# A backward list schedule that ranks every instruction by its latest start, in a planner that orders a two-layer decoder step

## The chip, the cores and the metric

The kernel runs on one core of one Trainium2 chip. The metric is the device time of one execution in microseconds (us), the median of several runs. A core has five engines that each work through a queue of their own in order: TensorE (PE) for matmuls and transposes, with its weight load shown apart as PEld; VectorE (DVE); ScalarE (ACT); GpSimd (POOL); and SyncE (SP), which here issues nearly all DMA transfers. An instruction waits at the head of its queue until what it needs is there, and everything behind it on that engine waits too.

## The reference

One inference step of a decoder with two layers, for a prompt of 2048 tokens and 8 sample tokens that share the weights; the width is 1024, all in float32:

```python
def even_mixer(x, past_kv, w_in, w_sp, b_sp):            # layer 0: branches A and B
    h = jnp.einsum('btd,de->bte', x, w_in)
    u, v, gate_a, q, k, vb, gate_b = _split(h, EVEN_SPLITS)
    u = jax.nn.gelu(u)
    v = _standardize(jax.nn.gelu(v)).astype(x.dtype)
    out_a = chunk_spatial_gate(u, v, w_sp, b_sp) * jax.nn.silu(gate_a)
    ...
    o = sweep_query_blocks(lambda qs, pos: stick_breaking(qs[0], keys, vals, pos, k_pos), (q,), q_pos)
    out_b = o.reshape(b, t, BRANCH_WIDTH) * jax.nn.silu(gate_b)
    return jnp.concatenate([out_a, out_b], axis=-1), new_kv, v

def odd_mixer(...):                                       # layer 1: branches C and D
    ...
    o = sweep_query_blocks(lambda qs, pos: dsa_attend(...), (q, q_idx, w_idx), q_pos)
    out_c = o.reshape(b, t, BRANCH_WIDTH) * jax.nn.silu(gate_c)
    out_d = multiscale_pool(p_ext, n_pref, q_pos, w_grp, scale) * jax.nn.silu(gate_d)
    return jnp.concatenate([out_c, out_d], axis=-1), new_kv, k_idx, new_buf

def post_norm(x, h, w_o, g, b):
    return _layer_norm(DN_ALPHA * x + jnp.einsum('bte,ed->btd', h, w_o), g, b)
```

`stick_breaking` is attention with 8 heads of 64 whose weights are running products of 1 − sigmoid(z) over the keys. `dsa_attend` lets an indexer with 4 heads of 32 score all keys, keeps the 256 best of each query, and does softmax attention over those with 8 query heads on 2 key heads and a relative bias. Both are causal for the prompt and read a paged cache for the samples. Each layer has one input projection, one output projection and a LayerNorm behind the residual.

## The kernel before

The prompt is worked on in 4 blocks of 512 tokens (TB), each of four tiles (P = 128 tokens). `Body` writes the program as generators for the stages and runs them interleaved, so that the order in which the code is written already mixes the stages of several blocks. What it writes is not what runs: `Order` takes the finished list of instructions, gathers what each depends on (`gather`), lays them on the five engines by a list schedule with planned durations (`cost`, `plan`), and pins the order that comes out on each engine (`keep`). In `plan` an instruction is ready when what it reads is done and its tile has a buffer; of the ready ones an engine takes the one that comes first in the program. The buffers of a tag (a name of a tile) are given out in program order. Waits between engines are set by the data alone; the planned durations are used only to choose the order.

The names in the rows below:

- `xc` are activations on their way in (a DMA on SP, L436); PE transposes them (`ps_x`, L439), and ACT and DVE split the result into a high part `xh` (L376) and a low part `xl` (L382). Weights `wr` (L387) are split in the same way into `wh` (ACT, L389) and `wl` (POOL and DVE, L392). A projection `pp` is three matmuls, high × high, low × high and high × low (L463 to L465). `q_hl` and `k_hl` are queries and keys after the same split by L382.
- Branch A: `wsp` are its four spatial weights (L507 to L511). Branch B: scores `z` (L753), a scan on DVE over `P` (L767), transposes `ps_p` (L790) and the sums `av` (L799).
- Branch C: the indexer's scores `z_i` (L1185), the search for the 256th best score (`tk_` names, to L1291), a mask `mk`. Then, for each tile of queries and each head, scores `z_c` of 128 queries by up to 512 keys in PSUM (L1495, two matmuls each). One DVE instruction (L1497) adds the mask, takes the largest (`mx`) and writes the sum as `zt` in SBUF, which frees the PSUM bank. ACT takes the exponential of `zt` (L1513). PE transposes it (`ps_pc`, L1526), ACT copies it back (L1528), and PE multiplies by the values into `av_c` (L1540, output tiles of 64 rows, the "halves" of the code). At the end of a tile of queries `c_sum` is scaled, multiplied by `av_c` and by the gate `gc` on DVE (L1564, L1568), and stored to `otd` on SP (L1571). The last tile is split instead (`lh`, `ll`).
- The output projection `pp_o` is again three matmuls, of `oh` and `ol` by the weights (L858 to L860, for the last tile L893 to L895); DVE adds it to the residual `xres` (L863, L897).
- LayerNorm (`ln_late`, `ln`): statistics, then for each of two halves of 512 columns and each of four tiles a multiply-add on DVE (L940), a product with `lng` on POOL (L941), a sum with `lnb` on DVE (L942), and the store (L909).

The scores `z`, `z_c` and `z_i` share one pool of two PSUM banks; `pp`, `ps_x`, `pp_o` and others share another; transposes a third.

Of the kernel before, what the change touches and what calls it, by code (L numbers as in the profile page):

```python
# [20 lines left out]
P = 128  # L21
# [34 lines left out]
class Order:  # L56

    ENGINES = {"PE": "PE", "DVE": "DVE", "Activation": "ACT", "Pool": "POOL", "SP": "SP"}
    SEM, DMA_START, DMA_END, RATE = 150, 700, 1500, 280.0

    def __init__(self, tc, lags):
# [44 lines left out]
    def gather(self):  # L106
# [3 lines left out]
        for n, i in enumerate(self.ins):  # L110
# [7 lines left out]
            for w, x in list(self.operands(i)):  # L118
# [74 lines left out]
    def cost(self, n):  # L193
# [22 lines left out]
        if e == "PE":  # L216
            k = self.size(i.outs[0])
            if i.is_transpose:
                return 90, 250
            if i.ins[0].dtype == F32R:  # L220
                return max(58, 0.444 * k), 0.444 * k + 170
            w = tuple(i.tile_size)[1] / P if self.halves(n) else 1.0
            return max(132, 1.7 * k * w), max(222, 1.7 * k) + 170
# [21 lines left out]
    def halves(self, n):  # L245
# [3 lines left out]
                and tuple(i.tile_size)[1] < P)  # L249


    def plan(self):

        N, eng, push, pop = len(self.ins), self.eng, heapq.heappush, heapq.heappop
        cost, halves = [self.cost(n) for n in range(N)], [self.halves(n) for n in range(N)]
        for g, ms in self.group.items():
            busy = sum(cost[m][0] for m in ms)
            cost[g] = busy, busy + 170
        dma = [e is not None and "DMA" in i.opcode for e, i in zip(eng, self.ins)]
        left, succ, tiles, home = [len(d) for d in self.dep], [[] for _ in range(N)], [[] for _ in range(N)], {}  # L260
        for n, d in enumerate(self.dep):
            for m in d:
                succ[m].append(n)
        for g, ts in self.tags.items():
# [8 lines left out]
        users = {t: len(u) for t, u in self.uses.items()}  # L273
        since, done = [0.0] * N, [0.0] * N
        ready, idle = {e: [] for e in self.ENGINES.values()}, dict.fromkeys(self.ENGINES.values(), 0.0)
        self.order = {e: [] for e in ready}
        due, back, now, dma_end, half, count = [], [], 0.0, 0.0, False, 0

# [6 lines left out]
        def take(g, t):  # L285
            while queue[g] and free[g] and open_[g]:
                x = queue[g].pop()
                free[g] -= 1
                open_[g] = False
                for n in self.uses[x]:  # L290
                    release(n, t)
# [6 lines left out]
        while count < N:  # L298
            while back and back[0][0] <= now:
                g = pop(back)[1]  # L300
                free[g] += 1
                take(g, now)
            while due and due[0][0] <= now:
                n = pop(due)[1]
                if eng[n] is not None:
                    push(ready[eng[n]], n)
                    continue
                count += 1
                for m in succ[n]:
                    release(m, now)  # L310
            moved = False
            for e, q in ready.items():
                while q and idle[e] <= now:
                    n = pop(q)
# [4 lines left out]
                    if dma[n]:  # L319
# [10 lines left out]
                    for t in tiles[n]:  # L330
# [7 lines left out]
                        if not users[t]:  # L338
                            push(back, (max(done[m] for m in u) + self.SEM, g))
# [4 lines left out]
        return max(done)  # L344

    def keep(self):
# [1839 lines left out]
def build(nc, shapes):  # L2186
    I = {n: nc.dram_tensor(n, s, d, kind="ExternalInput").ap() for n, s, d in shapes}
    O = {n: nc.dram_tensor("out_" + n, s, F32, kind="ExternalOutput").ap() for n, s in _OUTS}
    with tile.TileContext(nc, schedule_with_timeline_sim=True) as tc:
# [4 lines left out]
        order.gather()  # L2194
        order.plan()
        order.keep()
# [13 lines left out]
```

## Time and profile before

| | |
|---|---|
| median of 3 runs | 3044.42 us (3036.56 to 3045.0) |
| profiled execution | 3043.16 us |
| its span | 3041.5 us |
| mean granted clock of TensorE | 0.953 |
| PE busy | 2764.8 us |
| DVE busy | 2194.6 us |
| ACT busy | 1565.6 us |
| POOL busy | 1093.9 us |
| DMA | 523.50 MB, mean 172 GB/s |

The span runs from the first to the last instruction. The granted clock is what the throttle left of TensorE's full speed, as a mean over the span. In the views of the profile each row of waits has the engine and line that waited, what released it, the total us, how often, and the longest. A row of the timeline has the start, the duration, the engine and line, the operation with output and inputs, the number of instructions that the row holds together and, in brackets, how long the engine sat idle before it and what ended that.

### The profile page before, as it was taken

How to read it: one execution, taken by the hardware profiler on the slowest of the kernel's cores; microseconds unless marked ns; L12 is line 12 of the kernel's file. 1: busy time of each engine (PE TensorE's matmuls, PEld its weight loads, DVE VectorE, ACT ScalarE, POOL GpSimd, SP SyncE). 2: the span in 40 equal slices, each digit the busy share in tenths (PEclk: the TensorE clock that was granted, in tenths of full speed). 3: DMA queues.
4: the chain of work that ended last, by engine and by line, in shares of the span. 5: the costliest groups of instructions: out<-in, count | busy, mean ns of one | idle time of the engine just before them, and what ended most of it. 6: DMA issues, size and time to landing. Idle time of an engine off the chain costs nothing. (4 is left out here: it accounts for less than half of the span.)

```text
span 3041.5 us, 52342 instructions
## 1 busy us (share of the span) xinstructions
PE 2764.8 (91%) x17490; PEld 2189.1 (72%) x17490; DVE 2194.6 (72%) x5493; ACT 1565.6 (51%) x3148; POOL 1093.9 (36%) x1172
## 2 busy tenths in 40 slices
PE   7998999889999889979699999998899998988986
PEld 6886678667777767767477677767777887876875
DVE  2466557757775786548888988896888778778765
ACT  2433333334444334435366676774576675666842
POOL 2323235432324532242323422234322655434342
PEclk9999999999999999989799999998989998998998
DMA  7556866777585667454665555425555655665452
GB/s 215 161 177 205 256 185 184 241 215 211 163 259 160 204 212 233 128 151 115 178 166 148 143 140 148 114 74 152 161 156 140 198 179 169 201 201 180 125 171 66
DMA packets 536591, 523.50 MB, mean 172 GB/s; under 512 B 43183, under 2 KB 408904, under 8 KB 536287
## 3 DMA queue, kind: packets, MB, share of 16 engines
q1 hardware_dynamic: 526439, 484.29, 53.7%
q0 software_dynamic: 9856, 35.66, 3.7%
q8 instruction: 138, 2.26, 0.3%
q14 instruction: 158, 1.29, 0.1%
HBM read 430.27 MB, written 89.73 MB: 171 GB/s over the span
## 5 line engine op out<-in xcount | busy, mean ns | idle before, releaser
L392 POOL TENSOR_TENSOR wl<-wr,wh 128x512 fp32r<-128x512 f32 x260 | 411.5, 1583 | 972.6 <-ACT wh L389 884.7
L463 PE MATMUL pp<-xh,wh 128*128 128x512 f32 (+1 forms) x1536 | 636.2, 417 | 22.6 <-DVE q_hl L382 15.0
L464 PE MATMUL pp<-xl,wh 128*128 128x512 f32 (+1 forms) x1536 | 616.8, 402 | 0.1
L465 PE MATMUL pp<-xh,wl 128*128 128x512 f32 (+1 forms) x1536 | 613.1, 399 | 0.8 <-DMA ksc<-kcs 0.6
L389 ACT CAST wh<-wr 128x1024 fp32r<-128x1024 f32 x260 | 269.9, 1038 | 367.1 <-PE pp L464 202.8
L392 DVE TENSOR_TENSOR wl<-wr,wh 128x512 fp32r<-128x512 f32 x260 | 231.6, 891 | 199.3 <-ACT wh L389 183.5
L463 PEld LDWEIGHTS pp<-xh,wh 128*128 128x128 f32 (+1 forms) x1536 | 288.4, 189 | 101.7 <-issue 20.0
L465 PEld LDWEIGHTS pp<-xh,wl 128*128 128x128 f32 (+1 forms) x1536 | 289.4, 188 | 66.9 <-issue 7.4
L464 PEld LDWEIGHTS pp<-xl,wh 128*128 128x128 f32 (+1 forms) x1536 | 290.3, 189 | 63.9 <-issue 13.0
L858 PE MATMUL pp_o<-wh,oh 128*128 128x256 f32 x1008 | 300.9, 300 | 22.9 <-ACT oh L376 16.1
L860 PE MATMUL pp_o<-wh,ol 128*128 128x256 f32 x1008 | 291.9, 293 | 7.7 <-POOL ol L382 7.5
L859 PE MATMUL pp_o<-wl,oh 128*128 128x256 f32 x1008 | 291.5, 290 | 1.5 <-POOL wl L392 1.4
L767 DVE TENSOR_TENSOR_SCAN P<-P,bfst 128x512 f32<-128x512 f32 x192 | 265.8, 1392 | 35.4 <-ACT P L760 35.1
L1495 PE MATMUL z_c<-ksc,qc 128*128 128x512 f32 (+3 forms) x816 | 231.5, 370 | 65.0 <-DVE mx L1497 53.4
L791 ACT COPY P<-ps_p 128x512 f32<-128x512 f32 (+1 forms) x320 | 166.9, 523 | 184.4 <-PE ps_p L790 176.6
L1528 ACT COPY zt<-ps_pc 128x512 f32<-128x512 f32 (+3 forms) x320 | 164.1, 520 | 159.9 <-PE ps_pc L1526 154.1
L1513 ACT ACTIVATE zt<-zt,nmax 128x512 f32<-128x512 f32 (+3 forms) x320 | 208.4, 653 | 71.3 <-DVE nmax L1501 70.8
L858 PEld LDWEIGHTS pp_o<-wh,oh 128*128 128x128 f32 x1008 | 196.7, 195 | 34.4 <-ACT oh L376 17.8
L1482 POOL TENSOR_TENSOR nm<-nm,mk 128x256 f32<-128x256 f32 (+1 forms) x128 | 97.1, 760 | 342.8 <-DMA nm<-bft 158.5
L1495 PEld LDWEIGHTS z_c<-ksc,qc 128*128 128x128 f32 x816 | 141.7, 203 | 105.7 <-DVE mx L1497 65.1
L1241 ACT ACTIVATE mk<-ix,tk_tn 128x384 int8<-128x384 f32 (+13 forms) x140 | 183.4, 1310 | 54.9 <-DVE tk_tn L1291 30.3
L753 PE MATMUL z<-ks,q 128*128 128x512 f32 (+3 forms) x640 | 193.5, 390 | 13.2 <-ACT P L760 4.6
(456 smaller groups left out, 5913.5 us busy)
## 6 DMA issues: line engine op xcount, KB each, us to landing
pg<-cache_b_kv SPq DMA_DIRECT2D x256, 256.0 KB
wr<-w_in_even SPq DMA_DIRECT2D x112, 512.0 KB
wr<-w_in_odd SPq DMA_DIRECT2D x76, 512.0 KB
wr<-w_out SPq DMA_DIRECT2D x68, 512.0 KB
ks<-ksc SPq DMA_DIRECT2D x80, 256.0 KB
ksc<-kcs SPq DMA_DIRECT2D x80, 256.0 KB
q<-qsc SPq DMA_DIRECT2D x64, 256.0 KB
qc<-qcs SPq DMA_DIRECT2D x128, 128.0 KB
```

Source lines behind the costliest of these rows:

```text
L389: nc.scalar.copy(hi, raw)
L392: e.tensor_tensor(lo[:, c], raw[:, c], hi[:, c].bitcast(F32), op=OP.subtract)
L463: nc.tensor.matmul(ps[:m], wh[:, kt, :m], xh[kt], start=a, stop=False)
L464: nc.tensor.matmul(ps[:m], wh[:, kt, :m], xl[kt], start=False, stop=False)
L465: nc.tensor.matmul(ps[:m], wl[:, kt, :m], xh[kt], start=False, stop=b)
L753: nc.tensor.matmul(z[:, :n], q2[:, c, t * P:(t + 1) * P].bitcast(F32R), ks[:, :n].bitcast(F32R), start=c == 0, stop=c == 1)
L767: nc.vector.tensor_tensor_scan(r, r, r, initial=ini, op0=OP.mult, op1=OP.bypass)
L858: nc.tensor.matmul(ps[:, :256], oh[:, tt], wh[:, k], start=a, stop=False)
L859: nc.tensor.matmul(ps[:, :256], oh[:, tt], wl[:, k], start=False, stop=False)
L860: nc.tensor.matmul(ps[:, :256], ol[:, tt], wh[:, k], start=False, stop=b)
L1495: nc.tensor.matmul(z[:, :n], q2[:, c, jj % 2, :].bitcast(F32R), kk, start=c == 0, stop=c == 1)
L1513: nc.scalar.activation(zt, zt, AF.Exp, bias=nmx, accum_out=st["rs"][:, h, c:c + 1])
```

## The change

Four things change in `Order`; `Body` is untouched, and so are the instructions.

1. The planned durations: transposes 107 instead of 90 ns, float32r matmuls, halves and other matmuls a little different, POOL's tensor-tensor a bit longer with float32r output, and a figure of its own for a DVE tensor-scalar with two outputs.
2. On PE a change of kind (transpose, float32r, halves, other) costs the planner 45 ns, or 100 where halves are on one side. Before, only a change to or from halves cost 100.
3. Reads of one PSUM tile by the same engine keep their program order.
4. The plan is made three times. The first goes by program order, as before. Then `latest` runs a list schedule backwards from the end: every instruction is placed as late as its users, its engine and the buffers of the last plan allow. The starts that come out are the ranks by which the next forward plan chooses among ready instructions. The plan that the planner itself finds shortest is kept; here it is the one after the second backward pass.

```diff
@@ class Order
+    KIND, TILED = 45, 100
@@ gather: PSUM reads by the same engine
                 if w:
                     dep[n].update(m for m, g in rs if hit(g))
+                elif own and self.space(x) == PSUM:
+                    dep[n].update(m for m, g in rs if self.eng[m] == self.eng[n])
                     if own and self.space(x) != DRAM:
@@ cost
             if i.is_transpose:
-                return 90, 250
+                return 107, 270
             if i.ins[0].dtype == F32R:
-                return max(58, 0.444 * k), 0.444 * k + 170
...
+                return max(60 if tuple(i.tile_size)[1] < P else 88, 15 + 0.422 * k), 0.444 * k + 170
...
-            c = {"TensorTensor": 150 + 2.45 * k, "Iota": 50 + 0.9 * k, "Memset": 40}.get(i.opcode, 330 + 0.9 * k)
+            c = {"TensorTensor": 150 + (2.85 if i.outs[0].dtype == F32R else 2.4) * k, "Iota": 50 + 0.9 * k, "Memset": 40}.get(i.opcode, 330 + 0.9 * k)
...
+        elif i.opcode == "TensorScalarPtr" and len(i.outs) > 1 and len(full) == 1:
+            c = 150 + 1.05 * k
...
+    def settle(self):
...
+        best = self.plan(list(range(N))), self.order
+        for _ in range(2):
+            best = min(best, (self.plan(self.latest()), self.order), key=lambda x: x[0])
+        self.order = best[1]
...
@@ plan(self, rank)
-                    push(ready[eng[n]], n)
+                    push(ready[eng[n]], (rank[n], n))
...
-                    if e == "PE" and halves[n] != half:
-                        half = not half
-                        s += 100
+                    if e == "PE" and kinds[n] != kind:
+                        s += self.TILED if "h" in (kinds[n], kind) else self.KIND
+                        kind = kinds[n]
...
+    def latest(self):
...
+        for a in range(N):
+            for b in self.succ[a]:
+                edge(a, b, 1.0 if eng[a] == eng[b] == "PE" else lat[a] if eng[a] is not None else 0.0)
+        for t, u in self.uses.items():
...
+            for m in self.uses[self.after[t]] if t in self.after else ():
+                edge(m, u[0], lat[m])
...
+        def release(b):
+            for a, lag in pred[b]:
+                since[a] = max(since[a], start[b] + cost[b][0] + lag - cost[a][0])
+                left[a] -= 1
+                if not left[a]:
+                    push(due, (since[a], -a))
...
+        return [-s - c[0] for s, c in zip(start, cost)]
...
@@ build
-        order.plan()
+        order.settle()
```

`after` holds, for each tile, the tile whose buffer it took over in the last plan, so that the backward pass knows that the old tile's users must be done before the new one's first. The lines of `Body` move down by 86 (L1497 is now L1583, L940 is L1026).

What it moves is shown at three places. At the start, on SP, the queue begins before with two weights and constants:

```order
L387 DMA wr_110<-w_in_even 128x8x128
L387 DMA wr_117<-w_in_even 128x8x128
L957 DMA dsc_147<-d_scale 128x4x1
L959 DMA dwg_149<-d_w_grp 128x4x128
L1149 DMA tkc_165<-tk_const 128x32
L500 DMA pg_191<-page_table 1x128
L504 DMA bb_197<-a_b_sp 128x512
L507 DMA wsp_199<-a_w_sp 128x128
...
L1582 DMA x_smp_329<-x_sample 8x1024
L436 DMA xc_344<-x_prompt 128x4x128
```

and now:

```order
L593 DMA wsp_199<-a_w_sp 128x128
L593 DMA wsp_205<-a_w_sp 128x128
L593 DMA wsp_211<-a_w_sp 128x128
L473 DMA wr_110<-w_in_even 128x8x128
L593 DMA wsp_217<-a_w_sp 128x128
L522 DMA xc_344<-x_prompt 128x4x128
L1668 DMA x_smp_329<-x_sample 8x1024
L473 DMA wr_117<-w_in_even 128x8x128
L522 DMA xc_355<-x_prompt 128x4x128
L522 DMA xc_366<-x_prompt 128x4x128
```

The first activations xc_344 stand sixth instead of thirteenth, ahead of the second weight; four constants have gone behind.

In the middle of layer 1, at 2184 us of the profiled execution, DVE does a LayerNorm group for the block of `xres_27219` to `xres_27225`. Before, L1497 of two tiles of scores stands behind it:

```order
L942 TENSOR_TENSOR xres_27219<-xres_27219,lnb_28376 128x512
L940 TENSOR_SCALAR xres_27223<-xres_27223,ln_rs_28355,ln_nb_28373 128x512
L942 TENSOR_TENSOR xres_27221<-xres_27221,lnb_28376 128x512
L940 TENSOR_SCALAR xres_27225<-xres_27225,ln_rs_28355,ln_nb_28373 128x512
L942 TENSOR_TENSOR xres_27223<-xres_27223,lnb_28376 128x512
L1291 TENSOR_SCALAR tk_tn_28191<-tk_u3_28462,tk_wd_28459,tk_tn_28191 128x3
L1497 ISA zt_28592,mx8_28562<-z_c_28593,mk_27094 128x512
L1497 ISA mx8_28562 128x1
L942 TENSOR_TENSOR xres_27225<-xres_27225,lnb_28376 128x512
L1497 ISA zt_28613,mx8_28562<-z_c_28614,nm_28559 128x256
```

and now two such instructions stand behind the group's first row:

```order
L1026 TENSOR_SCALAR xres_27219<-xres_27219,ln_rs_28355,ln_nb_28373 128x512
L1583 ISA zt_28563,mx8_28562<-z_c_28564,mk_27094 128x512
L1583 ISA mx8_28562 128x1
L1583 ISA zt_28592,mx8_28562<-z_c_28593,mk_27094 128x512
L1583 ISA mx8_28562 128x1
L1026 TENSOR_SCALAR xres_27221<-xres_27221,ln_rs_28355,ln_nb_28373 128x512
L1026 TENSOR_SCALAR xres_27223<-xres_27223,ln_rs_28355,ln_nb_28373 128x512
L1026 TENSOR_SCALAR xres_27225<-xres_27225,ln_rs_28355,ln_nb_28373 128x512
```

z_c_28593 is taken ahead of most of the group; z_c_28614 follows fifteen rows later, behind most of its L1026. On PE the rows there were, before:

```order
L1540 MATMUL av_c_27082<-zt_28506,vsc_28159 64x128
L1526 MATMUL ps_pc_28655<-idf_81,zt_28533 128x128
L1540 MATMUL av_c_27082<-zt_28430,vsc_28235 64x128
L1540 MATMUL av_c_27082<-zt_28533,vsc_28235 64x128
L1495 MATMUL z_c_28680<-ksc_28550,qc_28556 128x512 x2
L1185 MATMUL z_i_28709<-kid_144,qi_28703 128x512
```

and are now:

```order
L1581 MATMUL z_c_28614<-ksc_28554,qc_28556 128x256 x2
L1612 MATMUL ps_pc_28512<-idf_81,zt_28305 128x128
L1959 MATMUL ps_sl_28605<-s_qb_27297,s_tmp_28545 128x16 x4
L1612 MATMUL ps_pc_28512<-idf_81,zt_28305 128x128
L1612 MATMUL ps_pc_28500<-idf_81,zt_28270 128x128 x3
L1581 MATMUL z_c_28680<-ksc_28550,qc_28556 128x512 x2
L1612 MATMUL ps_pc_28530<-idf_81,zt_28430 128x128
L1612 MATMUL ps_pc_28586<-idf_81,zt_28493 128x128 x4
L1612 MATMUL ps_pc_28619<-idf_81,zt_28506 128x128 x4
L1626 MATMUL av_c_27082<-zt_28270,vsc_28132 64x128
```

z_c_28680, which needs a bank that L1497 frees, now has transposes and the sums av_c of four tiles behind it, where it had z_i, which needs a bank too; z_i_28709 follows 23 rows later.

At the tail, on DVE, the last tile's c_sum stood between rows of the LayerNorm of the three tiles before it:

```order
L942 TENSOR_TENSOR xres_40528<-xres_40528,lnb_41648 128x512
L1564 TENSOR_TENSOR c_sum_41697<-c_sum_41697,av_c_27082 128x256
L942 TENSOR_TENSOR xres_40530<-xres_40530,lnb_41648 128x512
L1568 TENSOR_TENSOR c_sum_41697<-c_sum_41697,gc_41700 128x256
L942 TENSOR_TENSOR xres_40532<-xres_40532,lnb_41648 128x512
L382 TENSOR_TENSOR ll_41704<-c_sum_41697,lh_41703 128x256
```

and now:

```order
L1650 TENSOR_TENSOR c_sum_41697<-c_sum_41697,av_c_27082 128x256
L494 TENSOR_SCALAR rs_t_41592<-rs_t_41592 128x3
L489 TENSOR_SCALAR rs_t_41734<-rs_a_41733 8x1
L1654 TENSOR_TENSOR c_sum_41697<-c_sum_41697,gc_41700 128x256
L495 TENSOR_TENSOR ln_rs_41590<-ln_rs_41590,rs_t_41592 128x3
L490 TENSOR_SCALAR ln_rs_41732<-rs_t_41734 8x1
L949 SCALAR_TENSOR_TENSOR xres_40534<-xres_40534,pp_o_41480 128x256
L492 TENSOR_TENSOR rs_t_41592<-ln_rs_41590 128x3
L468 TENSOR_TENSOR ll_41704<-c_sum_41697,lh_41703 128x256
```

All three instructions on c_sum stand ahead of the group, whose first L1026 comes eleven rows after ll_41704.

More of the change, by code (lines that the diff above doesn't have):

```diff
@@ L249, in halves, with kind, plan @@
                 and tuple(i.tile_size)[1] < P)
-    def plan(self):
-        N, eng, push, pop = len(self.ins), self.eng, heapq.heappush, heapq.heappop
-        cost, halves = [self.cost(n) for n in range(N)], [self.halves(n) for n in range(N)]
-        for g, ms in self.group.items():
[L257 to L260, printed above, removed]
+    def kind(self, n):
+        i = self.ins[n]
+        if self.eng[n] != "PE" or type(i).__name__ != "InstMatmult":
+            return None
+        return "t" if i.is_transpose else "h" if self.halves(n) else "r" if i.ins[0].dtype == F32R else "f"
+    def settle(self):
+        N, eng = len(self.ins), self.eng
+        self.costs = [self.cost(n) for n in range(N)]
+        for g, ms in self.group.items():
+            busy = sum(self.costs[m][0] for m in ms)
+            self.costs[g] = busy, busy + 170
+        self.dma = [e is not None and "DMA" in i.opcode for e, i in zip(eng, self.ins)]
+        self.kinds = [self.kind(n) for n in range(N)]
+        self.succ = [[] for _ in range(N)]
         for n, d in enumerate(self.dep):
             for m in d:
-                succ[m].append(n)
+                self.succ[m].append(n)
+        best = self.plan(list(range(N))), self.order
+        for _ in range(2):
+            best = min(best, (self.plan(self.latest()), self.order), key=lambda x: x[0])
+        self.order = best[1]
+    def plan(self, rank):
+        N, eng, push, pop = len(self.ins), self.eng, heapq.heappush, heapq.heappop
+        cost, kinds, succ = self.costs, self.kinds, self.succ
+        left, tiles, home = [len(d) for d in self.dep], [[] for _ in range(N)], {}
         for g, ts in self.tags.items():
@@ L273, in plan @@
         users = {t: len(u) for t, u in self.uses.items()}
-        since, done = [0.0] * N, [0.0] * N
+        self.after, gone = {}, {g: [] for g in queue}
+        since, done, self.begun = [0.0] * N, [0.0] * N, [0.0] * N
         ready, idle = {e: [] for e in self.ENGINES.values()}, dict.fromkeys(self.ENGINES.values(), 0.0)
         self.order = {e: [] for e in ready}
-        due, back, now, dma_end, half, count = [], [], 0.0, 0.0, False, 0
+        due, back, now, dma_end, kind, count = [], [], 0.0, 0.0, None, 0
         def release(n, t):
@@ L287, in take @@
                 x = queue[g].pop()
+                if gone[g]:
+                    self.after[x] = gone[g].pop(0)
                 free[g] -= 1
@@ L299, in plan @@
             while back and back[0][0] <= now:
-                g = pop(back)[1]
+                _, g, x = pop(back)
                 free[g] += 1
+                gone[g].append(x)
                 take(g, now)
@@ L338, in plan @@
                         if not users[t]:
-                            push(back, (max(done[m] for m in u) + self.SEM, g))
+                            push(back, (max(done[m] for m in u) + self.SEM, g, t))
             if not moved:
@@ L344, in plan, with edge @@
         return max(done)
+    def latest(self):
+        N, eng, push, pop = len(self.ins), self.eng, heapq.heappush, heapq.heappop
+        cost = self.costs
+        lat = [c[1] + self.SEM + (self.DMA_START + self.DMA_END if d else 0) for c, d in zip(cost, self.dma)]
+        pred, left = [[] for _ in range(N)], [0] * N
+        def edge(a, b, lag):
+            pred[b].append((a, lag))
+            left[a] += 1
+        for a in range(N):
+            for b in self.succ[a]:
+                edge(a, b, 1.0 if eng[a] == eng[b] == "PE" else lat[a] if eng[a] is not None else 0.0)
+        for t, u in self.uses.items():
+            for m in u[1:] if self.tiles[t].space != DRAM else ():
+                edge(u[0], m, 0.0)
+            for m in self.uses[self.after[t]] if t in self.after else ():
+                edge(m, u[0], lat[m])
+        start, since = [0.0] * N, [0.0] * N
+        ready, idle = {e: [] for e in self.ENGINES.values()}, dict.fromkeys(self.ENGINES.values(), 0.0)
+        due, now, count = [(0.0, -n) for n in range(N) if not left[n]], 0.0, 0
+        heapq.heapify(due)
+        def release(b):
[4 more added lines that the diff above has]
+                    push(due, (since[a], -a))
+        while count < N:
+            while due and due[0][0] <= now:
+                n = -pop(due)[1]
+                if eng[n] is not None:
+                    push(ready[eng[n]], (-self.begun[n], -n))
+                    continue
+                start[n] = since[n]
+                count += 1
+                release(n)
+            moved = False
+            for e, q in ready.items():
+                while q and idle[e] <= now:
+                    n = -pop(q)[1]
+                    start[n], idle[e] = now, now + cost[n][0]
+                    count += 1
+                    moved = True
+                    release(n)
+            if not moved:
+                then = [due[0][0]] if due else []
+                then += [idle[e] for e in ready if ready[e]]
+                assert then or count == N
+                now = max([now] + [min(then)] if then else [now])
+        return [-s - c[0] for s, c in zip(start, cost)]
     def keep(self):
```

11 lines of the change are left out of this document (7 added, 4 removed).

## Prediction

> **What bounds the kernel now.** I read the page's header and shares first, then the clock, then the groups, and then what TensorE (PE) waited for.
>
> ```profile
> span 3041.5 us, 52342 instructions
> PE 2764.8 (91%) x17490; PEld 2189.1 (72%) x17490; DVE 2194.6 (72%) x5493; ACT 1565.6 (51%) x3148; POOL 1093.9 (36%) x1172
> ```
> ```profile
> core 0: 3041.5 us, clock 0.953
> ```
>
> PE is busy in 91% of the span, so all that an order of the same instructions can win is its idle time, 3041.5 − 2764.8 = 276.7 us, and the part of its busy time that a lower clock stretched. The clock stood at 0.953 on the mean: 0.047 × 2764.8 = 130 us of PE's work at the most. The profiled execution took 3043.16 us, 1.66 more than its span and 1.26 less than the median 3044.42; the sum below is made against 3043.16.
>
> What ended PE's idle time stands in the table of its waits (total us, times, longest):
>
> ```profile
> PE z_c L1495 <- DVE mx L1497: 53.4, 21, 10.2
> PE ps_x L439 <- DMA xc<-x: 24.2, 4, 17.3
> PE pp_o L858 <- ACT oh L376: 16.1, 5, 10.5
> PE pp L463 <- DVE q_hl L382: 15.0, 7, 6.1
> ...
> PE pp_o L893 <- ACT lh L376: 8.5, 1, 8.5
> PE ps_x L439 <- DMA xc<-x_prompt: 8.3, 4, 5.0
> PE ps_p L790 <- DVE xl L382: 8.1, 2, 7.9
> ...
> PE z_i L1185 <- DVE mx L1497: 7.4, 3, 7.0
> ...
> PE z L753 <- DVE mx L1497: 3.8, 6, 1.0
> ```
>
> Five of these rows wait for VectorE (DVE): 53.4 + 15.0 + 8.1 + 7.4 + 3.8 = 87.7 us. They are few and long, so I looked at one of them in the timeline, the 9.69 us at 2193.56:
>
> ```profile
> 2179.90 6.18 DVE L940 TENSOR_SCALAR xres<-xres,ln_rs,ln_nb 128x512 f32<-128x512 f32 x5
> 2180.07 8.80 POOL L941 TENSOR_TENSOR xres<-xres,lng 128x512 f32<-128x512 f32 x6 [1.76 <-DVE xres L940]
> ...
> 2183.43 0.19 PEld L1540 LDWEIGHTS av_c<-zt,vsc 128*64 128x64 f32 x2 [0.29 <-ACT zt L1528]
> ...
> 2187.67 1.48 DVE L940 TENSOR_SCALAR xres<-xres,ln_rs,ln_nb 128x512 f32<-128x512 f32 x1
> ...
> 2192.82 0.68 DVE L1497 CUSTOM_DVE_ANT_0 zt<-z_c,mk 128x512 f32<-128x512 f32 x1
> ...
> 2193.56 1.22 PE L1495 MATMUL z_c<-ksc,qc 128*128 128x512 f32 x2 [9.69 <-DVE mx L1497]
> ```
> ```profile
> L940 DVE TENSOR_SCALAR xres<-xres,ln_rs,ln_nb x64: 483/1479/1524, 562.4 to 3030.4; 128x512 f32<-128x512 f32 x64
> ```
>
> The LayerNorm of a block of four tokens' tiles is queued on DVE as one group: 8 of L940, each followed on POOL by L941 and again on DVE by L942. It holds DVE from 2179.90 to beyond 2191. The 0.68 us instruction L1497 that empties a bank of scores z_c stands behind it in DVE's queue, and PE cannot write the next scores until that bank is free. An L940 takes 0.48 us alone and 1.48 us at the median, while POOL runs L941; so a group is longer than its instructions look. The same picture, a group of L940 to L942 ahead of the instruction that frees a bank, stands before the other long waits:
>
> ```profile
> 1110.30 0.79 PE L463 MATMUL pp<-xh,wh 128*128 128x512 f32 x1 [6.06 <-DVE q_hl L382]
> ```
> ```profile
> 2574.49 0.79 PE L1185 MATMUL z_i<-kid,qi 128*128 128x512 f32 x1 [6.99 <-DVE mx L1497]
> ```
> ```profile
> 2766.26 1.22 PE L1495 MATMUL z_c<-ksc,qc 128*128 128x512 f32 x2 [10.17 <-DVE mx L1497]
> ```
> ```profile
> 2910.15 0.80 PE L1495 MATMUL z_c<-ksc,qc 128*128 128x256 f32 x2 [9.74 <-DVE mx L1497]
> ```
>
> **The change, part by part.** Nothing is added or removed on the chip: the same instructions stand on the same engines, in another order, and the planned durations exist only while the order is made. Every term is therefore a wait that goes, or one that comes.
>
> *LayerNorm groups, −45 us (0 to −85).* At 2184 PE now computes z_c_28593 and z_c_28614 earlier, the two L1497 for z_c_28564 and z_c_28593 stand ahead of five of the group's rows on DVE, and PE has transposes ps_pc and sums av_c left to run while DVE is in the group. But L1497 of z_c_28614 still stands behind most of it, so a part of the wait remains. What PE has there as filler is some 4 to 5 us by its durations: I take −5 of 9.69. At 2574 and at 2766 the order holds back more filler (output projection pp_o and av_c): −8 each, of 10.75 (6.99 and another 3.76 that follows from it) and 10.17. At 2910 −7 of 9.74, at 1110 −5 of 6.06, where q_hl's second half is moved ahead of the group. That is −33. At 575 (the 7.9 of xl) the order is as it was: 0, and one of the waits for q_hl, at 613, likewise (some 5 of the 15.0). The five places hold 42.7 of the 87.7 us (without the 3.76), the two unchanged ones some 13; some 32 us lie in short waits; latest starts put L1497 ahead of what nobody waits for, and I take 12 of them. The ends: nothing, if new waits of the same kind take their place; nearly all 87.7.
>
> *Start, −9 us (−4.8 to −13).*
>
> ```profile
> 0.81 1.07 SPq L387 DMA_DIRECT2D wr<-w_in_even  x2
> ...
> 5.64 2.08 SPq L507 DMA_DIRECT2D wsp<-a_w_sp  x4
> ...
> 8.22 1.48 SPq L436 DMA_DIRECT2D xc<-x_prompt  x3
> ...
> 12.80 1.97 PE L439 MATMUL ps_x<-idf,xc 128*128 128x128 f32 x8
> ...
> 14.59 1.22 PE L463 MATMUL pp<-xh,wh 128*128 128x512 f32 x2
> ...
> 25.25 1.94 PE L439 MATMUL ps_x<-idf,xc 128*128 128x128 f32 x8 [4.95 <-DMA xc<-x_prompt]
> ```
>
> Before, twelve loads go out on SP ahead of the first activations xc_344; afterwards five: four wsp at 2.08 / 4 and one wr at 1.07 / 2 us, so it is issued at 0.81 + 2.08 + 0.53 = 3.4 instead of 8.22. The first product pp follows 6.4 us behind that issue, at 9.8 instead of 14.59: −4.8. Its weights wr_110 are issued 1.6 us later than before, at 2.4, which is still 7 us ahead of that product. The xc whose lateness cost 4.95 at 25.25 now goes ahead of the second batch of weights: −4.2. The far end takes all 8.3 us of that row.
>
> *Loads that SP issues late, −3 us (−17 to +10).*
>
> ```profile
> 1476.67 0.37 SPq L1571 DMA_DIRECT2D otd<-c_sum  x1
> ...
> 1480.16 1.09 PE L439 MATMUL ps_x<-idf,xc 128*128 128x128 f32 x4 [17.33 <-DMA xc<-x]
> ```
>
> SP issues in its order; the store otd waited for DVE's c_sum behind a LayerNorm group, and the load xc behind it. Afterwards xc stands ahead of that store. It gains some 14 of 17.33. But the DVE instruction xl that takes xc's transposes now stands behind the same group, a new wait of some 11 us by the group's length less what goes ahead: −14 + 11. The 10.5 us for oh (at 1350, otd again late on SP) stay, the rows there are the same.
>
> *Tail, −5 us (0 to −8.5).*
>
> ```profile
> 3004.07 6.56 DVE L940 TENSOR_SCALAR xres<-xres,ln_rs,ln_nb 128x512 f32<-128x512 f32 x6
> ```
> ```profile
> 3014.79 0.58 PE L893 MATMUL pp_o<-wh,lh 128*128 128x256 f32 x1 [8.47 <-ACT lh L376]
> ```
>
> The last product waited 8.47 us, because c_sum and its split stood behind the six L940 on DVE. They now stand ahead of them. The group then runs beside the last product and meets the last tile's own LayerNorm, so I take 5 of 8.47.
>
> *Changes of kind on PE, +6 us (0 to +9.4).* Counted over both orders, PE goes from one kind of matmul to another 2259 times before and 2363 times now, 104 more.
>
> ```profile
> 1436.42 0.28 PE L859 MATMUL pp_o<-wl,oh 128*128 128x256 f32 x1
> 1436.54 0.28 PE L860 MATMUL pp_o<-wh,ol 128*128 128x256 f32 x1
> 1436.75 0.65 PE L799 MATMUL av<-P,vs 128*64 128x512 f32 x2
> ```
>
> A step between two of the same kind is 0.12 us here (from 1436.42 to 1436.54), the step to av 0.21: 0.09 more, and 104 × 0.09 = 9.4 if all are as dear.
>
> *New waits elsewhere, +22 us (0 to +60).* No trace of before shows them. Nearest are the waits that the groups cause now, some 10 us each; there are eight groups, two of which still wait as before. I take two new ones of 11, and as the end six of 10.
>
> *Clock, −14 us (0 to −58).* In two windows of equal length (us, then PE, PEld, DVE, ACT, POOL busy, the clock, DMA share, GB/s):
>
> ```profile
> 1400.00:1500.00 100.00, 69.33 (x407) 50.95 (x406) 80.61 (x218) 37.03 (x86) 28.47 (x30) 0.82 0.48 134
> 1900.00:2000.00 100.00, 99.28 (x668) 75.32 (x666) 86.68 (x256) 75.12 (x159) 28.74 (x41) 1.00 0.38 108
> ```
>
> Where PE idled 30.67 us the clock fell to 0.82, and up to 0.18 × 69.33 = 12.5 us of its work was lost, 0.41 us per idle us; over the span it is 130 / 276.7 = 0.47. Where PE did not idle the clock was 1.00. Net of the new waits 9 + 45 + 5 + 3 − 22 = 40 us of idling go. I take 0.35 of that, below both figures because some of the lost clock falls on time in which PE idles anyway. [...]
>
> Sum: −45 − 9 − 3 − 5 + 6 + 22 − 14 = −48; 3043.16 − 48 = 2995.
>
> **Rivals.** *The groups keep their length and the waits only change place.* The DVE work of a group is as long wherever it stands: 8 × 1.48 of L940, then L942. If PE's filler, put by for it, is run out, it waits for the next bank instead. The new waits then equal what the groups' term and the xc term win, the idle time and the clock stay, and start, tail and changes of kind remain: −9 − 5 + 6 = −8, 3035. For it speaks that z_c_28614's L1497 is behind the group still; against it that PE has filler in the order at three of the five places. [...]
>
> *Slower: scores run ahead, and their users come too close together.*
>
> ```profile
> L1495 PE MATMUL z_c<-ksc,qc 128*128 128x512 f32 (+3 forms) x816 | 231.5, 370 | 65.0 <-DVE mx L1497 53.4
> ...
> L1528 ACT COPY zt<-ps_pc 128x512 f32<-128x512 f32 (+3 forms) x320 | 164.1, 520 | 159.9 <-PE ps_pc L1526 154.1
> ```
>
> With z_c earlier and ps_pc and av_c later, the transposes, ACT's copy L1528 and the sums av_c of one tile follow each other directly, as ps_pc_28655 and av_c did before at 2183.43, where the copy was waited for 0.29 us. If each of 320 copies costs that, it is +93 us: 3088. From 48 / 320 = 0.15 us per copy on it outweighs the rest. For it speaks that the new order puts ps_pc in runs right ahead of their av_c; against it that ACT itself idled 154.1 us for ps_pc, so it takes a transpose at once, and that PE has a second and third transpose between in most rows.
>
> **How the numbers follow.** My forecast 0.71, waits only change place 0.13, scores ahead 0.16. The half widths of my forecast's terms are about 42, 4, 13, 4, 5, 30 and 20; taken together as independent they give 57, and since they are bounds and not likely values I take 40: 2955 to 3035. The range over all cases is 2945 to 3050, which leaves out some 0.04 below and 0.14 above, most of the slower rival. Within 0.3% means 9 us, about what a measurement of this kernel can tell from no change (its three runs lie within 8.4 us): 3035 to 3053. Faster: 0.67 of the forecast and 0.05 of the second case, which ends on that border; the same: 0.04 + 0.07 + 0.01; slower: the rest.
>
> **What would show it.** In the trace after, the wait of z_c for mx should fall from 53.4 to some 25 and no longer hold waits of 10 us; pp_o for lh at the tail should be gone; the first pp should stand near 10 and the first wait for xc_prompt should be short; ps_x for xc should be under 5 with ps_p or pp for xl, some 11, in its place; PE's idle time should be near 240 and the clock near 0.958. Wrong it is if PE's idle time is unchanged with other names (the second case), or if the waits of av_c and ps_pc for zt, too short for the rows above, grow to tens of us. What I could have wrong beyond these: SP's issues cost 0.3 to 0.5 us each in the rows above, and a load moved behind several others may come too late in a place I didn't look at.

## The result and the profile after

The changed kernel takes 2966.74 us (median of 4 runs, 2964.62 to 2968.68) against 3044.71 us for the kernel before, a ratio of 0.9735 (95% interval 0.970 to 0.977). Forecast were 2995, from 2945 to 3050.

The page of the kernel after, its header and shares, and its clock:

```profile
span 2962.9 us, 52295 instructions
...
PE 2747.0 (93%) x17490; PEld 2184.8 (74%) x17490; DVE 2163.9 (73%) x5493; ACT 1561.7 (53%) x3148; POOL 1112.2 (38%) x1172
```
```profile
core 0: 2962.9 us, clock 0.960
```

Of the 78.6 us by which the span is shorter, PE's idle time gave 60.8 (276.7 to 215.9) and its busy time 17.8. Each engine has as many instructions as before (the header's count also holds semaphore rows). ACT is as busy as before, DVE 30.7 us less and POOL 18.3 us more. PE's idle time falls into gaps between two matmuls and what follows the last one. Counted over all rows of PE, by the length of the gap:

| us (number) | before | after | difference |
|---|---|---|---|
| gaps of 4 us and more | 107.2 (12) | 43.1 (7) | −64.1 |
| 2 to 4 us | 41.5 (14) | 64.8 (21) | +23.3 |
| under 2 us | 108.2 (200) | 78.0 (152) | −30.2 |
| after the last matmul | 19.7 | 30.0 | +10.3 |
| PE busy | 2764.8 | 2747.0 | −17.8 |

So the long waits went, some came back as waits of 2 to 4 us, and the many short ones shrank by over a quarter. PE's waits after (total, times, longest):

```profile
PE z_c L1581 <- DVE mx L1583: 27.3, 19, 5.1
PE z_i L1271 <- DVE mx L1583: 11.9, 4, 5.6
PE pp_o L944 <- ACT oh L462: 11.8, 4, 8.9
PE z L839 <- DMA ks<-ksc: 10.8, 5, 3.9
PE ps_x L525 <- DMA xc<-x: 9.7, 7, 3.9
PE pp L550 <- DVE rs_t L494: 8.2, 1, 8.2
...
PE ps_so L2112 <- DVE s_acc L2115: 6.4, 1, 6.4
PE pp L549 <- DVE q_hl L468: 6.1, 3, 3.3
...
PE ps_x L525 <- DMA xc<-x_prompt: 5.4, 2, 4.3
...
PE ps_x L525 <- DVE xl L468: 2.5, 1, 2.5
```

z_c's wait for mx is halved (53.4 to 27.3), and no wait of 10 us is left. Four of the five LayerNorm places are still there, shorter; the timeline has the wait in brackets:

```profile
2134.18 0.80 PE L1271 MATMUL z_i<-kid,qi 128*128 128x512 f32 x1 [5.59 <-DVE mx L1583]
```
```profile
2501.02 0.79 PE L1271 MATMUL z_i<-kid,qi 128*128 128x512 f32 x1 [4.76 <-DVE mx L1583]
```
```profile
2687.63 1.87 PE L2112 MATMUL ps_so<-s_lg,s_pg 128*128 128x8 f32 x8 [6.36 <-DVE s_acc L2115]
```
```profile
2829.48 0.73 PE L1581 MATMUL z_c<-ksc,qc 128*128 128x512 f32 x2 [2.28 <-DVE mx L1583]
```

Where PE waited 9.69, 6.99 + 3.76, 10.17 and 9.74 us it now waits 5.59, 4.76, 6.36 and 2.28; at the fifth, 6.06 at 1110, no wait of 2 us is left. Together 46.4 us became 19.0.

**The place at 1480**, where PE had waited 17.33 us for xc, shows a wait cut in three:

```profile
1422.46 1.09 PE L525 MATMUL ps_x<-idf,xc 128*128 128x128 f32 x4 [3.21 <-DMA xc<-x]
...
1437.36 0.67 DVE L468 TENSOR_TENSOR xl<-ps_x,xh 128x512 fp32r<-128x512 f32 x1
1438.08 0.64 PE L550 MATMUL pp<-xl,wh 128*36 128x512 f32 x1 [8.16 <-DVE rs_t L494]
...
1443.87 0.45 PE L525 MATMUL ps_x<-idf,xc 128*128 128x128 f32 x1 [3.86 <-DMA xc<-x]
```

The load comes earlier, but xl stands behind the LayerNorm group, and PE waits 8.16 us for it. 3.21 + 8.16 + 3.86 = 15.2 us.

**The start.** SP's issues and PE's first products after:

```profile
2.19 0.43 SPq L473 DMA_DIRECT2D wr<-w_in_even  x1
...
3.29 0.43 SPq L522 DMA_DIRECT2D xc<-x_prompt  x1
...
8.47 0.48 PE L597 MATMUL ps_w<-idf,wsp 128*128 128x128 f32 x1 [3.72 <-POOL wsp L594]
...
8.88 1.02 PE L1672 MATMUL ps_xs<-idf,x_smp 8*128 8x8 f32 x8
...
11.62 0.80 PE L549 MATMUL pp<-xh,wh 128*128 128x512 f32 x1 [0.68 <-ACT xh L462]
...
16.62 0.38 SPq L522 DMA_DIRECT2D xc<-x_prompt  x1
...
22.59 1.09 PE L525 MATMUL ps_x<-idf,xc 128*128 128x128 f32 x4 [4.26 <-DMA xc<-x_prompt]
```

The first xc was issued at 3.29 as reckoned, 4.9 us earlier, but the first product came at 11.62 and not at 9.8, only 3.0 us earlier. In neither kernel do PE's rows ahead of that product show a wait for this xc. PE's queue waits for the spatial weights wsp, which POOL masks (until 10.12 before, until 8.47 now), and then transposes the sample's activations. Before, that row was:

```profile
10.12 0.72 PE L511 MATMUL ps_w<-idf,wsp 128*128 128x128 f32 x2 [10.12 <-POOL wsp L508]
```

The long wait, for the fourth xc, moved from 25.25 to 22.59 and stayed; SP issues that load at 16.62, where it had issued it at 18.93. Matched one by one, the matmuls at 50 to 250 us run only 1.1 us earlier than before. The windows of 5 to 30 us (us, PE, PEld, DVE, ACT, POOL busy, clock, DMA share, GB/s), before and after:

```profile
5.00:30.00 25.00, 14.60 (x59) 11.54 (x60) 5.32 (x9) 6.78 (x13) 5.67 (x8) 0.87 0.93 252
```
```profile
5.00:30.00 25.00, 15.85 (x61) 11.89 (x62) 5.59 (x9) 6.05 (x11) 4.97 (x5) 0.86 1.02 291
```

The DMA engines are full in both (a busy share of 0.93 and 1.02), so what is issued earlier shares them with everything else that was issued early.

**The tail.** The last product before ended at 3021.8 (its row first), and after (second fence) at 2932.9:

```profile
3021.49 0.28 PE L895 MATMUL pp_o<-wh,ll 128*128 128x256 f32 x1
```
```profile
2926.95 0.28 PE L979 MATMUL pp_o<-wh,lh 128*128 128x256 f32 x1
...
2932.59 0.28 PE L981 MATMUL pp_o<-wh,ll 128*128 128x256 f32 x1
...
2932.82 1.10 DVE L492 TENSOR_TENSOR rs_t<-ln_rs 8x1 f32<-8x1 f32 x1
...
2934.46 4.71 POOL L1027 TENSOR_TENSOR xres<-xres,lng 128x512 f32<-128x512 f32 x3 [0.55 <-DVE rs_t L493]
```

The wait of 8.47 us for lh is gone. But the group of three tiles that had filled that wait on DVE now runs behind the last product: DVE is busy for 20.2 us there instead of 10.3, POOL for 15.2 instead of 5.5. The end comes 30.0 us after that product instead of 19.7.

### The profile page after: what moved, and what is told of

Same layout as the page of the kernel before. It is cut to its first block, busy times and chain, and to the rows that moved or that the text cites. A ratio compares the mean times of both kernels' runs of the same rounds, so it can differ in the third digit from the quotient of the medians.

```text
span 2962.9 us, 52295 instructions
## 1 busy us (share of the span) xinstructions
PE 2747.0 (93%) x17490; PEld 2184.8 (74%) x17490; DVE 2163.9 (73%) x5493; ACT 1561.7 (53%) x3148; POOL 1112.2 (38%) x1172
## 5 line engine op out<-in xcount | busy, mean ns | idle before, releaser
L478 DVE TENSOR_TENSOR wl<-wr,wh 128x512 fp32r<-128x512 f32 x260 | 219.0, 843 | 210.7 <-ACT wh L475 190.0
L1581 PE MATMUL z_c<-ksc,qc 128*128 128x512 f32 (+3 forms) x816 | 222.0, 355 | 32.6 <-DVE mx L1583 27.3
L946 PEld LDWEIGHTS pp_o<-wh,ol 128*128 128x128 f32 x1008 | 197.1, 197 | 8.8 <-POOL ol L468 4.5
L945 PEld LDWEIGHTS pp_o<-wl,oh 128*128 128x128 f32 x1008 | 198.5, 197 | 5.2 <-issue 2.1
```

Of the source, the lines that this page charges most:

```text
L478: e.tensor_tensor(lo[:, c], raw[:, c], hi[:, c].bitcast(F32), op=OP.subtract)
L945: nc.tensor.matmul(ps[:, :256], oh[:, tt], wl[:, k], start=False, stop=False)
L946: nc.tensor.matmul(ps[:, :256], ol[:, tt], wh[:, k], start=False, stop=b)
L1581: nc.tensor.matmul(z[:, :n], q2[:, c, jj % 2, :].bitcast(F32R), kk, start=c == 0, stop=c == 1)
```

## The experiments

Each is compared with the kernel before on the same chip; ratios carry 95% intervals. The kernel after is 0.9735.

**Which part of the change wins: the durations or the ranks.** `costs_only` makes one plan in program order with the new durations; `ranks_only` has the old durations and the backward passes.

```diff
 costs_only:
-        best = self.plan(list(range(N))), self.order
-        for _ in range(2): ...
+        self.plan(list(range(N)))
 ranks_only: cost() as before, and
-                        s += self.TILED if "h" in (kinds[n], kind) else self.KIND
+                        s += 100 if "h" in (kinds[n], kind) else 0
```

> The kernel after, but planned once and by program order: the new durations, the price of a change of kind and the PSUM readers' order are there, the backward pass is not. Theory (the ranks win the time, because L1583 and its like come ahead of the LayerNorm groups): in this order L1580 of z_c still stands behind a whole group at 2184, and SP begins as before, so 3030 (3015 to 3050), with z_c's wait for mx at 45 to 60 us. Rival (the better durations win it): 2985 to 3000, with that wait under 35.

> The kernel after with the durations and the price of a change to halves as they were before, and two backward passes. Theory (ranks): 2975 (2955 to 2995). Rival (durations): 3015 to 3040.

`costs_only`: 3054.96 us, 1.0021 (1.0007 to 1.0034). `ranks_only`: 2993.29 us, 0.9818 (0.9798 to 0.9838). The ranks win; better durations alone lose a little, although z_c's wait for mx fell to 32.4 us, below what I had expected of this kernel. With the ranks the same durations are worth another 0.8% (0.9818 to 0.9735). A reading that fits, but that no run tests: planned durations that only decide when an instruction is ready in the plan do little, and as terms of a latest start they decide who goes first. Both kernels keep the third part of the change, the order of PSUM reads. With it the diff moves the two lines that forget covered reads and writes: they ran at a write, and now run at a read of a PSUM tile. Neither was run apart; `costs_only` shows only that they and the new durations win nothing without the ranks.

**Which engine's ranks.** `rank_pe` gives the latest starts to PE's queue alone, `rank_rest` to the four others.

```diff
+            late = self.latest()
+            late = [r if self.eng[n] == "PE" else n for n, r in enumerate(late)]    # rank_pe; != in rank_rest
```

> The kernel after, but the latest starts rank PE's queue alone; the other four engines choose by program order. Theory A (the win is on DVE, which takes the instruction that frees a PSUM bank ahead of LayerNorm and other work): little, 3035 (3015 to 3055). Theory B (the win is on PE, which runs scores early and keeps transposes and sums as filler): 2985 (2970 to 3005).

> The other half: DVE, ACT, POOL and SP choose by latest start, PE by program order. Theory A: 2985 (2970 to 3005). Theory B: 3035 (3015 to 3055). If both engines' orders must fit together, both halves lie over 3010.

`rank_pe`: 3027.88 us, 0.9936 (0.9915 to 0.9957). `rank_rest`: 3023.49 us, 0.9898 (0.9857 to 0.9939). Against `costs_only`, from which both differ by ranks alone, that is −0.85% and −1.2%, where both together win 2.9%: neither half has it. About a quarter of the gain, some 0.8%, needs both; by the intervals that can be 0.2 to 1.4%. Their pages show that they win different things (PE's line of `costs_only`, `rank_pe`, `rank_rest`):

```profile
PE 2774.8 (91%) x17490; PEld 2190.5 (72%) x17490; DVE 2197.5 (72%) x5493; ACT 1563.7 (51%) x3148; POOL 1100.8 (36%) x1172
```
```profile
PE 2756.3 (91%) x17490; PEld 2184.9 (72%) x17490; DVE 2188.8 (72%) x5493; ACT 1561.6 (52%) x3148; POOL 1100.2 (36%) x1172
```
```profile
PE 2775.6 (92%) x17490; PEld 2189.6 (72%) x17490; DVE 2180.6 (72%) x5493; ACT 1563.1 (52%) x3148; POOL 1103.8 (37%) x1172
```

| PE's gaps, us | costs_only | rank_pe | rank_rest | after |
|---|---|---|---|---|
| 4 us and more | 94.2 | 104.5 | 56.3 | 43.1 |
| 2 to 4 us | 46.0 | 41.7 | 64.1 | 64.8 |
| under 2 us | 117.4 | 101.1 | 105.3 | 78.0 |

The ranks on DVE and the rest take the long gaps, 38 us of them, of which 18 come back as gaps of 2 to 4 us. The ranks on PE take 18.5 us of PE's busy time and leave the long gaps alone. The short gaps fall by 12 to 16 us with either, and by 39 with both. Each column is one trace of one plan, though, and the short gaps differ much between plans of about the same time: `ln_price` below, with all ranks, has 109.4 us of them. So that row is a hint and no more.

**Whether the long gaps are the LayerNorm groups.** Two ways to shorten a group on DVE, each in the kernel before and in the kernel after: the multiply-add on ACT, or the three steps written as two on DVE with none on POOL.

```diff
 ln_act:
-                nc.vector.tensor_scalar(z, z, rs[:n, t:t + 1], nb[:n, t:t + 1], op0=OP.mult, op1=OP.add)
+                nc.scalar.activation(z, z, AF.Identity, bias=nb[:n, t:t + 1], scale=rs[:n, t:t + 1])
 ln_dve2, for all three lines:
+                nc.vector.scalar_tensor_tensor(z, z, mv[:n, t, 0:1], g[:n], op0=OP.subtract, op1=OP.mult)
+                nc.vector.scalar_tensor_tensor(z, z, rs[:n, t:t + 1], b[:n], op0=OP.mult, op1=OP.add)
```

> The kernel before with LayerNorm's multiply-add (L940) on ACT instead of DVE, one instruction for one; POOL's and DVE's other two stay. A group then holds DVE for about 8 x 0.9 = 7 us instead of some 15. Theory (what the ranks win is the waits behind LayerNorm groups on DVE): most of the five long waits go, 2995 (2980 to 3015). Rival (the groups are only where the waits happen to show, PE is short of ready work there anyway): 3030 to 3050.

> The kernel after with the same edit. Theory: the ranks have taken a good part of what the groups cost, so less than in the kernel before: 2945 (2925 to 2960). Rival (the two are additive, the ranks win elsewhere): as much as in before, 2915 to 2925 if before wins 45. If neither moves, the groups are not what matters: 2960 to 2975.

> The kernel after with LayerNorm's three steps written as two on DVE, (x - mean) * lng and x * rs + lnb, and none on POOL. A group holds DVE for 16 x 0.68 = 11 us instead of some 15 and waits for nobody. Theory (what is left of the cost is how long a group holds DVE): between the kernel after and the one with L1026 on ACT, 2956 (2948 to 2964). Rival (POOL running L1027 beside DVE is what costs, whoever does L1026): 2945 or less.

> The kernel before (its durations, its program order) with the same two-step LayerNorm on DVE and nothing of it on POOL. Theory A (the ranks win by getting round the LayerNorm groups): the groups cost before more than after, so this wins more than the 67 us that it won there, 2950 (2925 to 2970), and the ranks' own part shrinks from 78 to 25 to 70 us. Theory B (the ranks win elsewhere, in the short waits, and the two add): 67 us here too, 2978 (2970 to 2990).

Each of these kernels is planned anew, so its order differs in other places too.

| | LayerNorm as it was | ln_act | ln_dve2 |
|---|---|---|---|
| before | 1 | 0.9904 (0.9881 to 0.9927), 3018.78 us | 0.9808 (0.9786 to 0.9829), 2989.23 us |
| after | 0.9735 (0.970 to 0.977), 2966.74 us | 0.969 (0.9669 to 0.9711), 2952.37 us | 0.9513 (0.9492 to 0.9533), 2899.41 us |
| after / before, worked out | 0.9735 | 0.978 | 0.970 |
| gaps of 4 us and more, before | 107.2 | 49.4 | 48.4 |
| gaps of 4 us and more, after | 43.1 | 34.6 | 33.8 |

The last two rows show the theory right for what it speaks of. Shortening the groups takes the long gaps of the kernel before from 107 to 48 or 49 us, and the ranks take them to 43 with the groups' rows on DVE nearly as long (131.0 us before, 123.8 after). The waits of z_c for mx fall alike (`before_ln_dve2`, then `after_ln_dve2`):

```profile
PE z_c L1494 <- DVE mx L1496: 21.5, 20, 3.2
```
```profile
PE z_c L1580 <- DVE mx L1582: 21.8, 14, 5.5
```

But the third row refutes the theory as an account of the gain. If the groups were most of what the ranks win, the ranks would have little left to win where the groups are short. They win 2.2% and 3.0% there, about as much as with the old LayerNorm; `before_ln_dve2` lies where theory B had it, and `before_ln_act` between the two ranges. With `ln_dve2` the ranks take 28 us of short gaps (117.4 to 89.0), 12 of medium ones, 15 of long ones and 35.5 of busy time (2762.8 to 2727.3). And with ACT in the kernel before, 58 us fewer of long gaps shortened the span by only 22 us: short gaps grew from 108.2 to 124.3 and PE's busy time from 2764.8 to 2782.6.

`after_ln_dve2` is also the best kernel here, 67 us below the kernel after, where I had expected 11; nearer was the rival that POOL beside DVE is the cost. Its PE line and clock:

```profile
PE 2727.3 (94%) x17490; PEld 2165.8 (75%) x17490; DVE 2127.2 (73%) x5493; ACT 1560.4 (54%) x3148; POOL 1004.2 (35%) x1104
```
```profile
core 0: 2901.4 us, clock 0.973
```

Its span is 61.5 us below that of the kernel after: 29.7 us of gaps (185.9 to 156.2), 12 behind the last product, which ends 18 us before the end instead of 30, and 19.7 of busy time. The durations of LayerNorm's first step (min, median, max ns), in the kernel after and here:

```profile
L1026 DVE TENSOR_SCALAR xres<-xres,ln_rs,ln_nb x64: 526/720/3306, 552.1 to 2952.7; 128x512 f32<-128x512 f32 x64
```
```profile
L1026 DVE SCALAR_TENSOR_TENSOR xres<-xres,ln_mv,lng x64: 694/740/2165, 537.6 to 2895.9; 128x512 f32<-128x512 f32 x64
```

The medians are alike; what changed is the long rows. The first step takes 50.9 us in all against 63.3, DVE's two steps together 100.8 against 123.8, and DVE's other instructions 14 us less. What part POOL's free 108 us have in it was not tried apart.

**Whether truer prices give more.** `ln_price` gives the planner the measured durations of LayerNorm's three lines, `sp_price` 0.4 us for an issue on SP.

```diff
 ln_price:
+            c = {("DVE", "TensorScalarPtr"): 1020, ("Pool", "TensorTensor"): 1630, ("DVE", "TensorTensor"): 955}.get(...)
 sp_price:
-            return 65 if e == "SP" else 900, ...
+            return 400 if e == "SP" else 900, ...
```

> The kernel after with the measured durations of LayerNorm's three lines given to the planner (L1026 1.02 us instead of 0.46, L1027 1.63 instead of 1.38, L1028 0.955 instead of 0.81). If the waits that are left behind the groups come from the planner's belief that a group is short: 2950 (2935 to 2962). If the order around a group is as good as it gets: 2962 to 2975.

> The kernel after with SP's price of issuing a transfer at 0.4 us instead of 0.065 (the rows of SP show 0.3 to 0.5). If loads that stand behind others on SP cost PE time (xc 9.7, ks 10.8 and oh 11.8 us of waits are left): 2952 (2935 to 2962). If those waits come from the transfers themselves or from stores that wait: 2962 to 2980.

`ln_price`: 2975.29 us, 0.9758 (0.9719 to 0.9796). `sp_price`: 2970.88 us, 0.9738 (0.9701 to 0.9775). Neither differs from the kernel after. With LayerNorm's price PE waited less for mx (37.4 us in all rows instead of 43.8) and in gaps of 2 to 4 us (41.5 instead of 64.8), but longer in those under 2 us (109.4 instead of 78.0) and from 4 us on (50.3 instead of 43.1).

**The start and the tail.** `start_late_loads` tells the planner, by edges that only the plan sees, that nine early loads come after the first block's transposes; `tail_last_first` puts the last tile's projection and LayerNorm ahead of all else and gives its lng and lnb buffers of their own.

```diff
 start_late_loads:
+        for n in [n for n in sp if out(n) == "xres"][:4] + [n for n in sp if out(n) == "pg"][1:6]:
+            order.dep[n].add(xt)                        # the last transpose of xc in block 0
 tail_last_first:
+            late = [r - 1e7 * (n >= tail) for n, r in enumerate(self.latest())]
```

> The kernel after, in which the planner puts nine loads that nobody needs in the first block (the four residual rows xres of 512 KB and five pages pg of 256 KB) behind the transposes of the block's last activations. Theory (the start is bound by the DMA engines, which are fully busy from 5 to 30 us, so an earlier issue alone won next to nothing): the loads of xc land earlier, the waits for xc_prompt (5.4 us) go, 2960 (2955 to 2965). Rival (the start waits for weights and their split, or for the first transfers' own time): 2964 to 2972.

> The kernel after, in which the last tile's projection and LayerNorm go ahead of everything else that is ready, and its lng and lnb have buffers of their own and are loaded early. Theory (after the last product the end waits for DVE's group of the three other tiles and then for a load of lng, 30 us instead of 20 before): 10 us back, 2957 (2953 to 2963). Rival (DVE has the same rows to do whoever is first, and ends when it has done them): 2963 to 2970.

`start_late_loads`: 2960.66 us, 0.9713 (0.9694 to 0.9731). Its window of 5 to 30 us:

```profile
5.00:30.00 25.00, 21.36 (x119) 15.97 (x118) 8.15 (x13) 9.10 (x16) 5.92 (x6) 1.00 0.96 252
```

PE is busy for 21.36 instead of 15.85 us there, the clock stays at 1.00, and no wait for xc_prompt is left in the first 60 us. The matmuls at 50 to 250 us now run some 9 us earlier than in the kernel before, instead of 1.1. The rows of the fourth xc, for which PE had waited, show two causes:

```profile
12.84 0.37 SPq L522 DMA_DIRECT2D xc<-x_prompt  x1
...
17.02 0.60 PE L525 MATMUL ps_x<-idf,xc 128*128 128x128 f32 x4
```

SP issues it 3.8 us earlier, mostly since the loads of xres no longer stand ahead of it, and from its issue to its product it takes 4.2 us at the most instead of 6.0. So the early loads that nobody needs yet held up the start, by their place in SP's queue and by what they take of the DMA engines; the run moves both at once, and the queue's part is the larger for this load. The 6 us in the time fit, but the intervals of this kernel and of the kernel after overlap.

`tail_last_first`: 2965.37 us, 0.9724 (0.9704 to 0.9744), no different from the kernel after. Its last product ends 30.2 us before the end. The wait of 5.2 us for lng that the kernel after has there is gone, and the end comes no sooner: DVE is busy for 23.4 of the 30.2 us and POOL for 17.3, against 20.2 and 15.2 in the kernel after. Who goes first is not the matter; what is left to do behind that product is. With shorter rows (`after_ln_dve2`) 18 us are enough.

## Why the prediction was right, point by point

The direction and the range were right; the span fell by 78.6 us where 48 were forecast, and the time came out 28 us lower than 2995. In the classes of the table of gaps the steps of the forecast were: long waits −61 (LayerNorm places −33, xc −14, start −9, tail −5), new waits +33 (22, and 11 for xl), short waits and changes of kind −6, clock −14. Measured: −64, +23, −30, −18 in busy time, and +10 behind the last product, which the forecast did not have.

- *LayerNorm groups (−45).* For the long waits the mechanism is shown, by the order and by the runs that shorten the groups. The five places gave 27 us of the 33, with −4.1, −6.0, −3.8, −7.5 and about −6 against −5, −8, −8, −7 and −5. At one of the two places that I put at nothing 5 us went too (the 7.9 for xl is 2.5 now). The 12 for short waits was the term that was mis-sized: 30 went. And these are not the groups' doing: with short groups the ranks take as many (117.4 to 89.0). What takes them stays open; that PE's and the other engines' ranks must fit together rests on one trace of each half.
- *Start (−9).* Wrong: −1.1. One step that failed is that the first product follows the issue of its xc: it stood behind wsp in PE's queue, and came 3.0 us earlier where xc was issued 4.9 earlier. The other is the −4.2 for the fourth xc: issued 2.3 us earlier, it was still waited for (4.26 us instead of 4.95). The nine loads that nobody needs yet had to go for PE to gain 5.5 us of work there.
- *Loads on SP (−3).* Right with both halves: 17.33 became 15.2, with a new wait of 8.16 for xl where 11 were expected.
- *Tail (−5).* The wait went (−8.5), and about 1 us of the last product's own time (5.9 us instead of 7.0, at a granted clock of 1.00 instead of 0.61); the group that had hidden in it then cost 10.3 at the end. Net about +1. I took the group to run beside the last product, which lasts only 5.9 us.
- *New waits (+22).* That the gaps of 2 to 4 us grew by 23 is luck. The two waits of 11 us that I took as their form did not come (xl's 8.16 stands in another term), and some of these gaps are what is left of longer ones, such as the 3.21, 3.86 and 2.28 above.
- *Clock (−14) and changes of kind (+6).* The mean clock went from 0.953 to 0.960 and PE's busy time fell by 17.8, without the changes of kind being visible in it. How much of the 17.8 is the clock stays open. The matmuls' rows overlap, and busy time counts an overlap once. Added up row by row they last 5920.4 us before and 5915.5 after, so only 4.9 of the 17.8 are shorter rows and 12.9 are more overlap. With ranks on PE alone the busy time fell 18.5 us against `costs_only` at a clock of 0.955 instead of 0.953. There are 46 fewer gaps, and after each a matmul starts without the one before it running; that this is the cause was not tried.
- *Rivals.* That waits only change place fails on the gaps of 4 us and more, 107 to 43. That scores run ahead and their users come too close fails on ACT: PE's waits for ACT fell from 67.4 to 35.9 us in all. The groups' length changed little with the order, as the first rival had it: DVE's two steps took 131.0 us before and 123.8 after, and 100.8 when POOL was taken out. The median of the first step did fall, from 1479 to 720 ns, but a few rows grew to as much as 3306. That the length stays does not mean that the order wins nothing: the long gaps fell all the same.

## What to carry to other kernels

In an order that is planned, let each engine choose by the latest start from a backward pass, on all engines together; here PE alone was worth some 30% of it and the other engines some 43%, and better durations without it nothing. A latest start says nothing of bandwidth: a greedy forward plan still issues loads that nobody needs yet, and here, with the DMA engines full at the start (a busy share of 1.02 from 5 to 30 us), they held up the load that mattered. When a wait points at work that stands ahead in a queue, shorten that work too: the rewritten LayerNorm gave 67 us on top of the order's 78.

## What the runs showed of the hardware

Not only large rows of DVE took longer with a row of POOL beside them (in the kernel before L940 took 0.48 us at 3004.07, with none beside it, and 1.48 at the median). The tiny steps of the reciprocal root, 128x4 or smaller, did so too: one of them, L492, has a median of 156 ns in the kernel after and takes up to 1670 (min, median, max). That longest row, at 2668.98, has POOL's L468 for ol beside it, 1.29 us from 2669.32 on, and ends 0.04 us after that. The row at 2932.82 above is another of L492: it takes 1.10 us and ends with the L1027 that POOL began at 2932.65.

```profile
2932.65 1.26 POOL L1027 TENSOR_TENSOR xres<-xres,lng 128x512 f32<-128x512 f32 x1 [0.36 <-DVE xres L1026]
```
```profile
L492 DVE TENSOR_TENSOR rs_t<-ln_rs x33: 97/156/1670, 541.1 to 2948.5; 128x4 f32<-128x4 f32 x21, 8x1 f32<-8x1 f32 x6, 128x3 f32<-128x3 f32 x3, 128x1 f32<-128x1 f32 x3
```

I had counted this for the 512-wide rows alone. From the row at 2932.82 to the end five such small steps take 1.08 to 1.22 us each, 5.7 us in all, and each ends within 0.02 us of a row of L1027 on POOL. Not every step beside L1027 grows: five others start within POOL's row of 3.99 us at 2939.72 and take 0.13 or 0.14 us each, and the sixth takes 1.22. What sets them apart was not tried.
